# The order of SyncE's opening loads, the place of the key and query weights' measuring in layer 1, and the last tile's transposes one step later

## The chip, the cores and the metric

The kernel runs on one core of one Trainium2 chip. The metric is the device time of one execution in microseconds (us), the median of several runs. Names used below: PE is the tensor engine, ACT the scalar engine, DVE the vector engine, POOL the GpSimd engine, SP the sync engine, whose only work here is to issue DMA loads and stores. An engine with a q behind its name (SPq, ACTq) in the profile is that engine's instruction queue issuing a DMA.

## What is computed

Two layers of an encoder over 2048 tokens of width 1024, in float32. Each layer normalises the tokens, projects them with one combined matrix, mixes one half of the channels by a gated unit within chunks of 128 tokens and the other half by attention (8 query heads, 2 key/value heads, head width 64), projects back, normalises and adds.

```python
for l in range(DEPTH):
    h = rmsnorm(x, pre_g[l])
    proj = jnp.einsum('bsd,de->bse', h, w_in[l])
    u_a, v_a, g_a, q, k, v, g_b = jnp.split(proj, idx, axis=-1)
    y_a = gmlp_group(u_a, v_a, ln_a_g[l], ln_a_b[l], spatial_w[l], spatial_b[l]) * jax.nn.silu(g_a)
    y_b = gqa_axial_attention(q, k, v, q_norm_g[l], k_norm_g[l], tables) * jax.nn.silu(g_b)
    y = jnp.concatenate([y_a, y_b], axis=-1)
    out = jnp.einsum('bse,ed->bsd', y, w_out[l])
    x = x + rmsnorm(out, post_g[l])
```

`gqa_axial_attention` normalises queries and keys per head with `q_norm_g` and `k_norm_g`, rotates them by their row and column, and takes a softmax over all 2048 keys.

## The kernel before

**Numbers.** Every float32 operand of a matmul is split into a high and a low float16 part, and a product is three matmuls: high x high, low x high, high x low. A weight block has to be measured first (`split_steps`): its size gives a power of two, `w.e`, by which it is scaled before it is split. Measuring is done by a reduction of the raw block (`w_raw`) into columns of `w_col`; in the opening, half of it is done by squares on ACT instead, whose scratch result is called `fb`. Then come a small matmul `pe` that spreads the sum over the partitions, the scale `w_col<-g_col,w_col`, and eight pieces that write `w_hl`: high on ACT (or DVE), low on DVE (or POOL).

**Tokens.** The 2048 tokens are worked in 4 groups (`g`) of 4 tiles (`j`) of 128. A tile `x_t` is loaded, its squares are summed on ACT (`sq`, `ss_x`), a chain of tiny DVE instructions forms the reciprocal root (`rs_m` to `rs_x`; for two tiles at once `rr`), ACT scales one half of the tile and POOL the other, PE transposes it (`pt`), and ACT and DVE write the high and low half of `hT`. The projection matmuls are called `pp`.

**Order of blocks.** `run` goes through a list of blocks (weight block, group): first the two gate blocks `gb0` and `gb1` for each group, then keys and values with the first query block, and so on. Each call of `proj_tok` ticks a list of background jobs (`bg`) after each of its three passes of 8 matmuls; a job added with a delay of n runs at the n-th tick from then, at most 4 (later 2) to a tick. So a delay is a place in PE's program. In attention, `units` are pairs of a query tile and a key/value head; jobs hang on a step count `k` of 16 steps to a unit, 512 in all.

**Pinned and free instructions.** An instruction issued through the wrappers `PE`, `ACT`, `DVE`, `POOL` (class `Pinned`) keeps the place that the program gives it on its engine. One issued through `nc.vector`, `nc.scalar` or `nc.sync` is free: the scheduler may put it earlier or later in the engine's row. All SP loads are free before the change. Within its row each engine runs strictly in order. Each DMA sets one of eight completion semaphores, DMAHW0 to DMAHW7, that are handed round, and the next DMA on the same semaphore waits for it.

**The opening** is written out by hand at the end of `encoder` (line 1443 on): tile 0 and the gains of the pre-norm on SP, the first weight block (`w_first[0]`, two halves of 4 x 128 rows) on SP, the other three tiles of group 0 and the two halves of the second block on ACT's queue. Loads for group 1, the key weights and the six small loads of the query and key norm gains (`gains`, lines 249 to 259; three for each) come from background jobs of `run`, and `lng`, a gain of 512 elements of 4 bytes each, from `spatial_weights`.

**The boundary of the layers.** Layer 0's last tile is finished while layer 1's first projection already runs: `attend` ends by hanging its transposes `py`, its 12 products `pout` and its normalisation on background ticks 1 to 12 and later (line 1430 on). `o_tok` is that tile's attention result, divided by the softmax sums (`rden`). The measuring of layer 1's key and query weights (`split_w`, called by `split` in `run`) is free in layer 1 and pinned in layer 0. Layer 1's gains are asked for at step 256 of layer 0's attention and scaled (`scale_gains`, first instruction `g_top`) at step 268.

Of the kernel before, what the change touches and what calls it, by code (L numbers as in the profile page):

```python
# [19 lines left out]
P = 128  # L20
# [8 lines left out]
WB = 256  # L29
# [14 lines left out]
def encoder(ctx: ExitStack, tc, x, w_in, w_out, pre_g, post_g, ln_a_g, ln_a_b,  # L44
            spatial_w, spatial_b, q_norm_g, k_norm_g, rope, out):
    nc = tc.nc
# [43 lines left out]
            return f  # L90

    PE, ACT, DVE, POOL = Pinned(nc.tensor), Pinned(nc.scalar), Pinned(nc.vector), Pinned(nc.gpsimd)

    ident = const.tile([P, P], F32, name="ident")
    make_identity(nc, ident)
# [103 lines left out]
    class Project:  # L199
# [10 lines left out]
        def norm_row(self):  # L210

            self.g_col = lay.tile([P, ND], F32, name="g_col")
            self.g_row = f_t("fa")[0:ND, 0:P]
            nc.sync.dma_start(self.g_row, pre_g[self.l].rearrange("(d p) -> d p", p=P))

        def norm_turn(self):

# [4 lines left out]
        def begin(self):  # L222

            self.w_first = [Obj(), Obj()]
            steps = []
            for n, w in enumerate(self.w_first):
                raw = w_t([P, ND, WB], "w_raw", F32)

                def load(i, raw=raw, c=C_GB + n * WB, queue=ACT if n else nc.sync):
                    ds4 = slice(4 * i, 4 * i + 4)  # L230
                    queue.dma_start(raw[:, ds4], w_in[self.l, 4 * i * P:(4 * i + 4) * P, c:c + WB]
                                      .rearrange("(d p) e -> p d e", p=P))
                steps.append(([load], self.split_steps(w, raw, sums=4)))
            return steps
# [15 lines left out]
        def gains(self):  # L250
            l = self.l
            self.gain_q = lay.tile([P, 2, HD], F32, name="gain_q")
            self.gain_k = lay.tile([P, 2, HD], F32, name="gain_k")
            for gain, src in ((self.gain_k, k_norm_g), (self.gain_q, q_norm_g)):
                nc.sync.dma_start(gain[:, 0, :], src[l].partition_broadcast(P))
                gv = gain[:, 1, :].rearrange("p (a h i) -> p a h i", a=2, h=2)
                sv = src[l].rearrange("(a h i) -> a h i", a=2, h=2)
                for h in range(2):
                    nc.sync.dma_start(gv[:, :, h, :], sv[:, 1 - h, :].partition_broadcast(P))

        def scale_gains(self, v):
            top = small.tile([P, 2], F32, name="g_top")
# [12 lines left out]
        def spatial_weights(self):  # L275
            l = self.l
            self.lng = lay.tile([P, 4], F32, name="lng")
            nc.sync.dma_start(self.lng, ln_a_g[l].rearrange("(t p) -> p t", p=P))
            self.zbias = lay.tile([P, 4, P], F32, name="zbias")
            wsT = row_t("wsT")  # L280
            self.ws = row_t("ws", (P, 2, NH * P), F16)
            sq = small.tile([P, 4], F32, name="ws_sq", bufs=1)
            for hf in range(2):
                raw = f_t("fa")
                nc.sync.dma_start(raw.rearrange("p (g j) -> p g j", g=4),
                                  spatial_w[l, 4 * hf:4 * hf + 4].rearrange("g i j -> i g j"))

                def t(hf=hf, raw=raw):
                    ps = ps_t("pt")
                    for g in range(4):  # L290
                        PE.transpose(ps[:, g * P:(g + 1) * P], raw[:, g * P:(g + 1) * P], ident)
                    nc.scalar.copy(wsT[:, hf * GRP:(hf + 1) * GRP], ps)
                    nc.scalar.activation(raw, raw, AF.Square, accum_out=sq[:, hf:hf + 1])
                bg.add(WS_DELAY + 2 * hf, t)

            def scale():
                nc.vector.tensor_scalar(sq[:, 2:3], sq[:, 0:1], sq[:, 1:2], W_SPREAD, ALU.add, ALU.mult)
                ps = ps_t("pe")
                PE.matmul(ps[:, 0:1], ones, sq[:, 2:3], start=True, stop=True)
                top_scale(sq[:, 2:3], ps[:, 0:1], nc.vector, float(157 << 23))  # L300
                nc.vector.tensor_scalar(sq[:, 3:4].bitcast(I32), sq[:, 2:3].bitcast(I32), -1.0, float(254 << 23),
                                        ALU.mult, ALU.add)
                nc.vector.tensor_scalar(self.lng, self.lng, sq[:, 3:4], 1.0 / V_SCALE, ALU.mult, ALU.mult)

            def split(hf):
                sl = slice(hf * GRP, (hf + 1) * GRP)
                nc.scalar.activation(self.ws[:, 0, sl], wsT[:, sl], AF.Copy, scale=sq[:, 2:3])
                nc.vector.scalar_tensor_tensor(self.ws[:, 1, sl], wsT[:, sl], sq[:, 2:3], self.ws[:, 0, sl],
                                               ALU.mult, ALU.subtract)
            bg.add(WS_DELAY + 10, scale)  # L310
            for hf in range(2):
                bg.add(WS_DELAY + 20 + 4 * hf, lambda hf=hf: split(hf))
            lnb = f_t("fb")
            nc.sync.dma_start(lnb, ln_a_b[l].partition_broadcast(P))
            sb = f_t("fc").rearrange("p (c i) -> p c i", c=4)
            for h in range(2):
                src = spatial_b[l].rearrange("(c h) i -> h c i", h=2)[h]
                nc.sync.dma_start(sb[h * HD:(h + 1) * HD], src.partition_broadcast(HD))

            def bias():  # L320
                ps = ps_t("pt").rearrange("p (c i) -> p c i", c=4)
                for c in range(4):
                    for h in range(2):
                        e = (2 * c + h) * HD
                        PE.matmul(ps[h * HD:(h + 1) * HD, c], lnb[:, e:e + HD], wsT[:, 2 * e:2 * e + P],
                                  start=True, stop=True)
                nc.vector.tensor_tensor(self.zbias, ps, sb, ALU.add)
            bg.add(WS_DELAY + 14, bias)
# [96 lines left out]
        def hT_jobs(self, g):  # L425
# [4 lines left out]
            act, dve = (nc.scalar, nc.vector) if done else (ACT, DVE)  # L430
            parts = small.tile([P, TPG, 2], F32, name="ss_x", bufs=2)

            def load(j, queue=nc.sync):
                if done:
                    src = h_d[(g - 1) * TPG + j]
                    xs[j] = xt = [f_t("x_h") for _ in range(2)]
# [307 lines left out]
        def run(self, kv, first, last_jobs, first_wo):  # L744
# [42 lines left out]
                raws[name] = self.load_w(cols[name])  # L787

            def split(name, delay):
                w[name] = self.split_w(raws.pop(name), delay, self.l == 0 and name in ("kv", "q0"))  # L790

            def block(name, g):
                assert all(w[n].ready for n in (("va0", "va1") if name == "va" else (name,)))
# [117 lines left out]
    def attend(l, kv, nxt):  # L911
# [500 lines left out]
        def run(fs):  # L1412
            for f in fs:
                f()
# [16 lines left out]
        run(post_queue)  # L1431
        for n, f in enumerate(gb_pieces):
            bg.add(1 + n, f)
        bg.add(1, trans)
        bg.add(1, split)
        bg.add(4, lambda: run(mms[0] + after[0] + gain_part(s, 0, POOL)))
        bg.add(7, lambda: run(mms[1] + after[1] + gain_part(s, 1, POOL)))
        bg.add(10, lambda: run(posts[:4]))
        bg.add(11, lambda: run(posts[4:8]))
        for n, f in enumerate(posts[8:]):  # L1440
            bg.add(12 + n, f)

    layers = [Project(l) for l in range(DEPTH)]
    pj = layers[0]
# [3 lines left out]
    (loads, steps), (loads2, steps2) = pj.begin()  # L1448
    loads[0](0)
    loads[0](1)  # L1450
    pj.norm_turn()
    jobs.squares(0)
    for j in range(1, TPG):
# [4 lines left out]
    jobs.scale(0, z)  # L1458
    steps[2]()
    banks = [jobs.turn(0, 0)]  # L1460
    loads2[0](0)
    jobs.squares(1)
    steps[3]()
    banks.append(jobs.turn(0, 1))
# [8 lines left out]
    z = jobs.chain(1)  # L1473
    for d in (ND - 2, ND - 1):
        w.low(d, POOL)
    loads2[0](1)
    jobs.squares(2)
    jobs.scale(1, z)
    jobs.squares(3)
# [61 lines left out]
```

## Time and profile before

| | us |
|---|---|
| median of 3 runs | 2470.33 (2467.57, 2470.33, 2476.21) |
| the profiled execution | 2471.2 |
| its span, first to last instruction | 2469.2 |
| PE busy | 2414.1 (98%) |
| DVE / ACT / POOL busy | 1742.6 / 1639.0 / 1192.8 |
| granted PE clock, mean | 0.997 |
| DMA, mean rate | 76 GB/s |

The page divides the span into 40 slices of some 62 us; PE is at nine tenths or more in all but the first and the last two. A busy share is an average, so the stretches in which PE is not busy have to be looked for. The views used below: busy time by stretch (one line has, after the stretch and its length, busy us and instruction count of PE, PE's weight loads, DVE, ACT and POOL, then the granted clock, the DMA engines' share and GB/s); waits (who waited for whom: us in total, times, longest); and the timeline (start, length, engine, line, operation, output<-inputs; in brackets the idle time before it and what ended that). Line 89 is the wrapper of pinned instructions, so there the tile names tell which instruction it is.

### The profile page before, as it was taken

The page shows a single profiled execution, that of the slowest core. Times are in us where ns is not written, and L with a number is a line of the kernel's source. Part 1 is how long each engine was busy: PE and PEld are TensorE (multiplying, and loading weights), DVE is VectorE, ACT ScalarE, POOL GpSimd, SP SyncE. Part 2 cuts the span into 40 slices and gives each one's busy share as a digit, 9 for nine tenths or more (in the row PEclk, how much of TensorE's full clock was granted, in tenths as well). Part 3 has the DMA queues.
Part 4 walks back from the last instruction along what each step waited for, and adds up shares of the span by engine and source line. Part 5 has one row for each costly group of instructions (what it writes and reads, how often), then busy time and mean ns, then how long its engine had stood idle before and what let it go on. Part 6 is the DMA issues. An engine that isn't in the chain of part 4 may idle for free. (4 is left out here: it accounts for less than half of the span.)

```text
span 2469.2 us, 62843 instructions
## 1 busy us (share of the span) xinstructions
PE 2414.1 (98%) x25327; PEld 1600.1 (65%) x25327; DVE 1742.6 (71%) x4001; ACT 1639.0 (66%) x3545; POOL 1192.8 (48%) x1000
## 2 busy tenths in 40 slices
PE   5999999999999999999999999999999999999997
PEld 4988776445666666666579987764456666666664
DVE  5678566876678777777766875678667777777674
ACT  5665323247888888888854742231588888888886
POOL 2200110026777777777731111100477777777776
PEclk9999999999999999999999999999999999999999
DMA  5353213222121222111144422221321121212120
GB/s 175 123 175 89 59 49 92 61 80 73 52 92 40 62 66 70 60 48 64 57 150 147 144 69 69 74 62 57 107 66 38 50 61 42 68 43 68 51 68 27
DMA packets 174916, 188.11 MB, mean 76 GB/s; under 512 B 19608, under 2 KB 143648, under 8 KB 174624
## 3 DMA queue, kind: packets, MB, share of 16 engines
q1 hardware_dynamic: 173136, 181.47, 24.2%
q8 instruction: 198, 3.24, 0.5%
q10 hardware_dynamic: 1488, 2.62, 0.3%
q14 instruction: 94, 0.77, 0.1%
HBM read 129.38 MB, written 54.66 MB: 75 GB/s over the span
## 5 line engine op out<-in xcount | busy, mean ns | idle before, releaser
L89 POOL TENSOR_TENSOR p_parts<-p_f,p_parts 128x512 f16<-128x512 f32 x872 | 1034.2, 1198 | 331.5 <-ACT p_f L89 252.3
L89 ACT ACTIVATE p_parts<-sp 128x512 f16<-128x512 f32 x1024 | 620.2, 606 | 173.6 <-PE sp L89 125.4
L89 PEld LDWEIGHTS <-p_parts 128*128 128x128 f16 x12288 | 509.5, 97 | 249.7 <-POOL p_parts L89 6.5
L89 DVE TENSOR_REDUCE mx<-pmax 128x1 f32<-128x512 f32 x800 | 541.6, 684 | 177.1 <-PE pmax L89 174.0
L89 PE MATMUL pp<-w_hl,hT 128*128 128x256 f16 x5376 | 619.6, 274 | 5.4 <-ACT w_hl L89 5.0
L89 ACT ACTIVATE p_f<-sp 128x512 f32<-128x512 f32 x1024 | 617.7, 603 | 0.0
L89 PEld LDWEIGHTS <-hT 128*128 128x128 f16 x5376 | 526.3, 98 | 72.5 <-issue 3.5
L89 PE MATMUL po<-v_st,p_parts 128*128 128x65 f16 (+1 forms) x12288 | 542.4, 193 | 6.8 <-POOL p_parts L89 4.5
L89 PE MATMUL pout<-wo,y_t 128*128 128x512 f16 x1536 | 488.0, 378 | 1.7 <-ACT y_t L89 1.7
L89 PE MATMUL sp<-q,k_t 66*128 66x512 f16 x1024 | 390.0, 381 | 0.0
L89 PE MATMUL sp<-q_st,k_t 128*128 128x512 f16 x1024 | 387.8, 379 | 1.6 <-DVE o_tok L89 1.3
L89 PE MATMUL pmax<-k_t,q_m 128*128 128x512 f16 x1024 | 386.9, 379 | 0.8 <-DVE mx L89 0.4
L89 PE MATMUL pp<-hT,w_hl 128*128 128x512 f16 x1536 | 370.3, 379 | 0.0
L89 PEld LDWEIGHTS <-y_t 128*128 128x128 f16 x1536 | 148.9, 97 | 177.7 <-ACT y_t L89 3.3
L89 PEld LDWEIGHTS <-w_hl 128*128 128x128 f16 x1536 | 149.7, 98 | 174.0
L89 PEld LDWEIGHTS <-q_m 128*128 128x128 f16 x1024 | 101.1, 99 | 120.7
L971 DVE TENSOR_REDUCE mx<-pmax 128x1 f32<-128x512 f32 x224 | 150.3, 686 | 36.9 <-PE pmax L89 36.7
L89 POOL TENSOR_TENSOR wo<-wo_raw,wo 128x512 f16<-128x512 f32 x32 | 37.1, 1158 | 263.9 <-ACT wo L89 150.4
L89 DVE TENSOR_TENSOR p_parts<-p_f,p_parts 128x512 f16<-128x512 f32 x152 | 118.5, 780 | 36.8 <-ACT p_f L89 35.9
L628 POOL TENSOR_TENSOR fl<-fv,fh 128x512 f16<-128x512 f32 x32 | 38.0, 1206 | 205.7 <-ACT fh L627 197.0
L89 PEld LDWEIGHTS <-k_t 128*128 128x128 f16 (+1 forms) x2048 | 131.3, 97 | 3.8 <-DVE o_tok L89 1.4
L546 ACT ACTIVATE fc<-pp,rs_y 128x64 f32<-128x64 f32 x320 | 69.9, 355 | 69.5 <-DVE rs_y L123 69.5
(212 smaller groups left out, 2041.2 us busy)
## 6 DMA issues: line engine op xcount, KB each, us to landing
w_raw<-in_w_in_dram SPq DMA_DIRECT2D x10, 1024.0 KB
w_raw<-in_w_in_dram SPq DMA_DIRECT2D x18, 512.0 KB
gb_d<-fa SPq DMA_DIRECT2D x32, 256.0 KB
wo_row<-in_w_out_dram SPq DMA_DIRECT2D x16, 512.0 KB
wo_raw<-in_w_out_dram SPq DMA_DIRECT2D x16, 512.0 KB
z_d<-fb SPq DMA_DIRECT2D x32, 256.0 KB
fb<-z_d SPq DMA_DIRECT2D x32, 256.0 KB
ya_d<-fa SPq DMA_DIRECT2D x32, 256.0 KB
```

The lines of the kernel that those rows point to most:

```text
L89: return tc.keep_in_program_order(call(*args, **kw))
L546: nc.scalar.activation(qn[:, t, h], src[:, t, h], AF.Copy, scale=rs[:, i, t, h:h + 1])
L628: nc.gpsimd.tensor_tensor(s.lo, vh, s.hi, ALU.subtract)
L971: dve.tensor_reduce(s.mx[:, j, c:c + 1], ps, AX.X, ALU.max)
```

## The change

Three edits and what they bring along:

1. A fifth wrapper, `SP`, pins loads on the sync engine: the pre-norm gains, both first weight blocks (the second moves from ACT's queue to SP's), the query and key norm gains, `lng`, and the token tiles of groups 0 and 1 in layer 0. In the opening, both halves of the second weight block are issued directly behind those of the first.
2. The key weights' and first query block's measuring and splitting is pinned in layer 1 too.
3. The last tile's transposes, products and normalisation at the boundary come one background tick later.

```diff
+    SP = Pinned(nc.sync)
...
-            nc.sync.dma_start(self.g_row, pre_g[self.l].rearrange("(d p) -> d p", p=P))
+            SP.dma_start(self.g_row, pre_g[self.l].rearrange("(d p) -> d p", p=P))
...
-                def load(i, raw=raw, c=C_GB + n * WB, queue=ACT if n else nc.sync):
+                def load(i, raw=raw, c=C_GB + n * WB, queue=SP):
...
             for gain, src in ((self.gain_k, k_norm_g), (self.gain_q, q_norm_g)):
-                nc.sync.dma_start(gain[:, 0, :], src[l].partition_broadcast(P))
+                SP.dma_start(gain[:, 0, :], src[l].partition_broadcast(P))
...
-                    nc.sync.dma_start(gv[:, :, h, :], sv[:, 1 - h, :].partition_broadcast(P))
+                    SP.dma_start(gv[:, :, h, :], sv[:, 1 - h, :].partition_broadcast(P))
...
-            nc.sync.dma_start(self.lng, ln_a_g[l].rearrange("(t p) -> p t", p=P))
+            SP.dma_start(self.lng, ln_a_g[l].rearrange("(t p) -> p t", p=P))
...
-            def load(j, queue=nc.sync):
+            def load(j, queue=SP if self.l == 0 and g < 2 else nc.sync):
...
-                w[name] = self.split_w(raws.pop(name), delay, self.l == 0 and name in ("kv", "q0"))
+                w[name] = self.split_w(raws.pop(name), delay, name in ("kv", "q0"))
...
-        bg.add(1, trans)
-        bg.add(1, split)
-        bg.add(4, lambda: run(mms[0] + after[0] + gain_part(s, 0, POOL)))
-        bg.add(7, lambda: run(mms[1] + after[1] + gain_part(s, 1, POOL)))
-        bg.add(10, lambda: run(posts[:4]))
-        bg.add(11, lambda: run(posts[4:8]))
+        bg.add(2, trans)
+        bg.add(2, split)
+        bg.add(5, lambda: run(mms[0] + after[0] + gain_part(s, 0, POOL)))
+        bg.add(8, lambda: run(mms[1] + after[1] + gain_part(s, 1, POOL)))
+        bg.add(11, lambda: run(posts[:4]))
+        bg.add(12, lambda: run(posts[4:8]))
         for n, f in enumerate(posts[8:]):
-            bg.add(12 + n, f)
+            bg.add(13 + n, f)
...
     loads[0](0)
     loads[0](1)
+    loads2[0](0)
+    loads2[0](1)
     pj.norm_turn()
...
     banks = [jobs.turn(0, 0)]
-    loads2[0](0)
     jobs.squares(1)
...
-    loads2[0](1)
     jobs.squares(2)
```

SP's row from the start of the program, before, with the semaphores that a load waits for (`x_t` a token tile, `fa` the pre-norm gains, `w_raw` a weight block: 128x4x256 half of one of the first two, 128x8x256 the whole key block):

```order
L442 DMA x_t<-in_x_dram 128x1024
L214 DMA fa<-in_pre_g_dram 8x128
L231 DMA w_raw<-in_w_in_dram 128x4x256 x2
L255 DMA gain_k<-in_k_norm_g_dram 128x64
L259 DMA gain_k<-in_k_norm_g_dram 128x2x16 x2
L255 DMA gain_q<-in_q_norm_g_dram 128x64
L259 DMA gain_q<-in_q_norm_g_dram 128x2x16 [waits DMAHW0_49]
L259 DMA gain_q<-in_q_norm_g_dram 128x2x16 [waits DMAHW1_49]
L278 DMA lng<-in_ln_a_g_dram 128x4x1 [waits DMAHW2_49]
L442 DMA x_t<-in_x_dram 128x1024 [waits DMAHW6_49]
L442 DMA x_t<-in_x_dram 128x1024 [waits PE_49,DMAHW0_49,Activation_49,Pool_49]
```

The same place of the change:

```order
L89 DMA x_t<-in_x_dram 128x1024
L89 DMA fa<-in_pre_g_dram 8x128
L89 DMA w_raw<-in_w_in_dram 128x4x256 x4
L89 DMA x_t<-in_x_dram 128x1024 [waits DMAHW1_49]
L339 DMA w_raw<-in_w_in_dram 128x8x256 [waits DMAHW2_49]
L89 DMA x_t<-in_x_dram 128x1024 [waits DMAHW0_49,PE_49,DMAHW3_49,Activation_49,Pool_49]
L89 DMA gain_k<-in_k_norm_g_dram 128x64 [waits DMAHW4_49]
L89 DMA gain_k<-in_k_norm_g_dram 128x2x16 [waits DMAHW5_49]
L89 DMA gain_k<-in_k_norm_g_dram 128x2x16 [waits DMAHW6_49]
L89 DMA gain_q<-in_q_norm_g_dram 128x64 [waits DMAHW7_49]
```

The second weight block has moved up, the six gain loads have moved behind two tiles of group 1 and the key weights, and `lng` is gone from here.

ACT's row in the opening, before, behind the squares of tile 0 (`fb` is the measuring of the first weight half; the last row belongs to tile 1):

```order
L89 DMA x_t<-in_x_dram 128x1024 [waits DMAHW3_49]
L89 DMA x_t<-in_x_dram 128x1024 [waits DMAHW4_49]
L89 DMA x_t<-in_x_dram 128x1024 [waits DMAHW5_49]
L89 ACTIVATE fb,w_col<-w_raw,g_col 128x256 [waits DMAHW2_49,DVE_49]
L89 ACTIVATE fb,w_col<-w_raw,g_col 128x256 x3
L89 ACTIVATE x_t<-x_t,rs_x 128x512 [waits DVE_49]
L89 DMA w_raw<-in_w_in_dram 128x4x256 [waits DMAHW7_49]
L89 ACTIVATE sq,ss_x<-x_t 128x512 [waits DMAHW3_49]
```

And of the change:

```order
L89 DMA x_t<-in_x_dram 128x1024 x3
L89 ACTIVATE fb,w_col<-w_raw,g_col 128x256 [waits DMAHW2_49,DVE_49]
L89 ACTIVATE fb,w_col<-w_raw,g_col 128x256 x3
L89 ACTIVATE x_t<-x_t,rs_x 128x512 [waits DVE_49]
L89 ACTIVATE sq,ss_x<-x_t 128x512 [waits DMAHW6_49]
```

The three tile issues wait for no semaphore of another load any more, and the weight issue between them and tile 1's squares is gone.

DVE's row at the boundary of the layers, before (`rs_m`, `rs_o` begin the normalisation of the last tile but one; `rden` to `o_tok` finish the last tile):

```order
L89 TENSOR_SCALAR rs_o<-rs_m 128x1
L357 TENSOR_REDUCE w_col<-w_raw 128x4 x2
L361 TENSOR_TENSOR w_col<-w_col,g_col 128x8
L362 TENSOR_REDUCE w_col<-w_col 128x1
L368 TENSOR_SCALAR w_col<-w_col 128x1
L89 TENSOR_SCALAR rden<-po,cols 128x4
L89 RECIPROCAL rden<-rden 128x4
```

And of the change:

```order
L89 TENSOR_SCALAR rs_m<-ss_o,cols 128x1
L89 TENSOR_SCALAR rs_o<-rs_m 128x1
L89 TENSOR_SCALAR rden<-po,cols 128x4
L89 RECIPROCAL rden<-rden 128x4
L89 TENSOR_TENSOR gb<-gb,rden 128x2x2x64
```

The measuring of the key weights has left this place; it now stands after the first two gate products of layer 1 for group 0, ahead of group 1's token chain. Two more moves have no rows here: layer 1's six gain loads now stand in SP's row behind the `gb` load of step 256 of layer 0's attention (before, they stood among the projections of layer 0), and `lng` stands in each layer directly ahead of the loads for the spatial bias and the first rotation rows (`rope`).

## The prediction

> **What bounds the kernel now.** I read the page first, then busy time by stretch, then what the tensor engine waited for, then the timeline where it waited.
>
> ```profile
> span 2469.2 us, 62843 instructions
> PE 2414.1 (98%) x25327; PEld 1600.1 (65%) x25327; DVE 1742.6 (71%) x4001; ACT 1639.0 (66%) x3545; POOL 1192.8 (48%) x1000
> ...
> 0.00:50.00 50.00, 23.66 (x148) 17.60 (x149) 26.90 (x89) 26.79 (x68) 10.41 (x14) 0.95 0.59 192
> 100.00:200.00 100.00, 100.00 (x927) 90.31 (x925) 70.19 (x245) 59.98 (x168) 15.18 (x10) 1.00 0.48 146
> 1200.00:1300.00 100.00, 94.38 (x1053) 72.14 (x1052) 62.35 (x155) 69.47 (x147) 48.00 (x41) 1.00 0.36 117
> ```
>
> The first number after a stretch's length is PE busy. PE works through the whole program except in two places that this change touches: 26 of the first 50 us, and 5.6 us around the boundary of the layers. An edit elsewhere can only cost; an edit here is worth the PE idle time that it removes, since PE then works at 100% behind it.
>
> ```profile
> PE pt L89 <- ACT x_t L89: 15.3, 3, 13.1
> PE pp L89 <- ACT w_hl L89: 5.0, 3, 3.0
> ...
> PE py L89 <- DVE o_tok L89: 2.7, 1, 2.7
> ```
>
> PE's longest wait is 13.1 us for the first token tile, scaled on ACT; the 2.7 us are the last tile's transposes at the boundary. The opening, in order of time (start, length, engine; in brackets idle before and its end):
>
> ```profile
> 0.73 0.39 SPq L442 DMA_DIRECT2D x_t<-in_x_dram  x1
> ...
> 2.57 0.51 SPq L255 DMA_DIRECT2D gain_k<-in_k_norm_g_dram  x1
> ...
> 4.23 0.60 ACT L89 ACTIVATE sq<-x_t 128x512 f32<-128x512 f32 x1 [2.22 <-DMA x_t<-in_x_dram]
> ...
> 5.52 0.19 ACT L89 ACTIVATION_READ_ACCUMULATOR sq<-x_t 128x1 f32 x1
> ...
> 7.67 0.37 SPq L278 DMA_DIRECT2D lng<-in_ln_a_g_dram  x1
> ...
> 9.01 5.53 ACTq L89 DMA_DIRECT2D x_t<-in_x_dram  x3
> 9.01 1.22 DVE L89 TENSOR_REDUCE w_col<-w_raw 128x4 f32<-128x1024 f32 x1 [1.20 <-DMA w_raw<-in_w_in_dram]
> ...
> 14.64 0.51 ACT L89 ACTIVATE fb<-w_raw,g_col 128x256 f32<-128x256 f32 x1 [8.94 <-DMA x_t<-in_x_dram]
> ...
> 16.63 0.71 ACT L89 ACTIVATE x_t<-x_t,rs_x 128x512 f32<-128x512 f32 x1
> ...
> 17.39 1.11 PE L89 MATMUL pt<-ident,x_t 128*128 128x128 f32 x4 [13.06 <-ACT x_t L89]
> ...
> 19.33 0.23 DVE L89 TENSOR_SCALAR w_col<-g_col,w_col 128x8 f32<-128x8 f32 x1
> ...
> 20.25 0.60 ACT L89 ACTIVATE sq<-x_t 128x512 f32<-128x512 f32 x1 [2.91 <-DMA x_t<-in_x_dram]
> ...
> 22.10 0.91 ACT L89 ACTIVATE w_hl<-w_raw,w_col 128x256 f16<-128x256 f32 x2
> ...
> 24.12 0.20 DVE L89 TENSOR_SCALAR rs_m<-ss_x 128x1 f32<-128x1 f32 x1
> ```
>
> ACT is free at 5.71 us. Next in its order stand three issues of token tiles, and each waits for the semaphore of a load issued eight loads earlier: the second weight half (landed at 9.01, when DVE's reduction starts) and two of the small gain loads. So ACT measures the first weight half (fb) only at 14.64, though that half had landed by 7.67: the lng issue waits for its semaphore. The DMA engines were not the reason:
>
> ```profile
> 9.00:10.00 1.00, 0.00 (x0) 0.00 (x0) 0.99 (x1) 0.00 (x0) 0.56 (x1) 1.00 0.06 7
> ...
> 17.00:18.00 1.00, 0.61 (x3) 0.62 (x4) 0.38 (x2) 0.34 (x1) 0.00 (x0) 1.00 0.89 353
> ```
>
> The last two numbers are the DMA share and GB/s: 7 GB/s in the stall, 353 in a full microsecond.
>
> **The opening, step by step.** The written SP order has no gain load ahead of the token tiles, so ACT's three issues wait for nothing. They begin at 5.71 and take 3 x 0.43 = 1.3 us, to 7.0. fb then starts when its half lands, 7.65: 7.0 us earlier than 14.64. Its squares, the scaling of the tile and PE's first transposes move by the same 7.0 (17.39 to 10.4); DVE's reduction stays at 9.01 and is done in time. The weight scale, ready at 19.56, is ready at 12.6. ACT's squares of tile 1, which waited 2.91 us for its load, can begin at 10.35, so ACT's first w_hl goes from 22.10 to 12.6. DVE's four w_hl take 1.55 us and the two low halves of hT 0.69 each: DVE reaches the second tile's chain at 15.6 instead of 24.12, which is **8.5 us**. What follows waits for DVE and ACT in a pinned order, not for loads, and keeps that distance.
>
> The condition is tile 1's landing. Squares to chain take 24.12 - 20.25 = 3.87 us, so it may land as late as 11.7; each later microsecond costs one. The bounds: tile 0 took 3.5 us from issue to landing (0.73 to 4.23), which gives 9.2; tile 1 before took 11.2 us (9.01 to 20.25), which gives 16.9 and leaves 3.3 us of gain. I take the near end, since the long one fell into the idle DMA microseconds quoted. Counted by bytes: tile 0 and the first weight block are in by 9.0; tile 1 and as much of the second block are 1.05 MB, 3 us at 353 GB/s, so 12 if nothing of them had moved before, and about 11 since both stand in the queues by then.
>
> On this a rule bears: the Trainium skill, "DMA: Bandwidth & Descriptors", section "Issuing engines are not separate DMA queues", says that loads issued on ACT and SP run on the same 16 DMA engines, so that a second issuing engine saves only issue time. By it the second weight block's move to SP is worth nothing, and its 1 MB, now issued ahead, competes with tile 1; the sum would be the same 8.5 with shared bandwidth, less with the tile behind the block. No row before has both.
>
> The moves that I cost at nothing, with their cover. The six gain loads go behind the second tile of group 1; their first reader was at 59.6 us, DVE's scale_gains, and three such loads take some 7 us (below). The second block's ACT issues (0.4 us each) vanish beside a waiting ACT.
>
> **The clock.** The granted clock (the number before the DMA share) is not full in the opening:
>
> ```profile
> 36.00:40.00 4.00, 4.00 (x29) 3.28 (x28) 1.78 (x3) 2.52 (x8) 0.00 (x0) 0.76 0.35 115
> 48.00:52.00 4.00, 3.82 (x20) 2.66 (x20) 2.89 (x17) 3.97 (x13) 0.00 (x0) 0.57 0.17 57
> ```
>
> Lost there: 4 x 0.24 + 4 x 0.43 = 2.7 us. The same gaps between the same matmuls stay, so I take no change, with 2 us either way. The Trainium skill, "TensorE: Matmul & The Clock Gate", section "Part 1: The HAM clock gate (the "warmup" mystery)", has the activity window run free, so the same gaps can meet it otherwise; that fits a term without a sign.
>
> **The boundary.**
>
> ```profile
> 1240.02 7.23 SPq L338 DMA_DIRECT2D w_raw<-in_w_in_dram  x2
> ...
> 1246.35 0.83 PE L89 MATMUL po<-v_st,p_parts 128*128 128x65 f16 x12
> 1246.49 2.34 DVE L357 TENSOR_REDUCE w_col<-w_raw 128x4 f32<-128x1024 f32 x2 [2.54 <-DMA w_raw<-in_w_in_dram]
> ...
> 1249.40 0.21 DVE L89 TENSOR_SCALAR rden<-po,cols 128x4 f32<-128x4 f32 x1
> ...
> 1250.32 0.42 DVE L89 TENSOR_TENSOR o_tok<-po,gb 128x256 f32<-128x256 f32 x1
> ...
> 1250.80 0.44 PE L89 MATMUL py<-ident,o_tok 128*128 128x128 f32 x2 [2.74 <-DVE o_tok L89]
> ```
>
> DVE had put the measuring of layer 1's key weights ahead of the last tile: it waited for them, reduced them, and reached rden at 1249.40, while po was complete at 1247.2. Pinned, the measuring stands after the first projection block. rden to the end of o_tok takes 1.34 us, so o_tok is ready at 1248.6. PE runs 16 matmuls (2.1 us from 1247.0) instead of 8 ahead of the transposes, to 1249.1: no wait, **2.7 us** gained, and 0.5 spare. Were the extra tick handed on to the product of the last tile, 1.0 of it would go, so 1.7 to 2.7. The pinned splits of layer 1 then alternate with transposes as layer 0's already do, where PE was busy 100.00 of 100 us.
>
> The gain loads of layer 1 now stand in the middle of layer 0's attention, behind this gb load; the second fence is three of them and the DMA rate after:
>
> ```profile
> 893.15 0.35 SPq L1284 DMA_DIRECT2D gb<-gb_d  x1
> ...
> 924.64 0.34 DVE L89 TENSOR_REDUCE g_top<-gain_k 128x1 f32<-128x64 f32 x2
> ```
>
> ```profile
> 417.11 1.30 SPq L255 DMA_DIRECT2D gain_q<-in_q_norm_g_dram  x1
> 418.46 0.94 SPq L259 DMA_DIRECT2D gain_q<-in_q_norm_g_dram  x2
> ...
> 423.00:424.00 1.00, 1.00 (x10) 0.82 (x9) 0.69 (x1) 0.00 (x0) 0.00 (x0) 1.00 0.06 7
> ```
>
> The trickle lasts from 417 to 424, 7 us for three, so 14 for six: landed by 908, read at 924.64, 17 us spare. The q loads behind them serve step 272, four after g_top's, and have the same cover. Nothing. lng, now in front of the rope rows, delays these; they had slack:
>
> ```profile
> 1357.01 1.27 POOL L528 TENSOR_TENSOR fa<-fa,gain_k 128x512 f32<-128x512 f32 x1 [35.39 <-DMA fa<-in_rope_dram]
> ...
> 1363.20 0.43 DVE L548 TENSOR_TENSOR fc<-fc,fa 128x256 f32<-128x256 f32 x1 [0.39 <-ACT fc L546]
> ```
>
> POOL ends at 1358.3, DVE reads at 1363.2: 4.9 us of cover, so nothing, at worst 2 us a layer by a trickle of 7 us.
>
> **The sum.** 8.5 + 2.7 = 11.2 us off the profiled execution's 2471.2 us (span 2469.2 and 2.0 around it) gives **2460.0**. That execution is 0.9 us above the median, 2470.33; the three timed runs spread over 8.6 us.
>
> **Rivals.** One, the issue itself is slow:
>
> ```profile
> L89 ACTq DMA_DIRECT2D x_t<-in_x_dram x3: 387/434/3510, 9.0 to 11.0; - x3
> ```
>
> One of ACT's three issues took 3.51 us in itself. If the group takes 5.53 us again, from 5.71, fb starts at 11.3, 3.3 us earlier; with tile 1 there by then, DVE's chain starts at 19.3 instead of 24.12: 4.8, and 2463.7 in all. For it: that issue shows no wait of its own. Against: the gain loads were then unfinished, and SP's issues take 0.4.
>
> Two, tile 1 comes late, behind the second weight block on the shared engines: it lands at 16.9, the opening gives 3.3, the total is 6.0: 2465.2.
>
> Three, slower than before: the gain loads in mid-attention hold SP. If each of the six holds the queue for 7.23 us, as the pair of loads at 1240.02 did, the last is issued at 893.5 + 43 = 937 and lands 2.3 us later (7 us for three), at 939; DVE stands 15 us at scale_gains, with the maxima and subtractions that PE needs behind it, and the sum is 2471.2 - 11.2 + 15 = 2475. It costs from a landing past 924.6 on, makes the kernel slower than before past 936, and by over 0.3% past 943; 14 us of trickle were measured where 31 are free, so it is unlikely.
>
> Four, nothing of it shows: other waits close up behind both places, 2471.
>
> **Chances.** Forecast 0.60, slow issue 0.15, late tile 0.14, nothing 0.06, slower 0.05 (one in five of that within 0.3%). The range goes from 2455 (clock and spread on the good side) to 2468 (the late tile, with the spread). A measurement of this kernel tells about 0.3% from no change, 7.4 us: below 2462.9 is faster. That takes nearly all of the forecast and part of rivals one and two: faster 0.68, same 0.28, slower 0.04.
>
> **What would show it.** In the opening: ACT's three issues directly behind the squares of tile 0, fb near 7.7, PE's first transposes near 10.4, tile 1's squares with no wait, PE's first pp near 13. At the boundary: no measuring between rs_o and rden on DVE, py without idle time ahead. In attention: g_top without a wait for a gain load. Wrong it would be if fb started after 10 us, if DVE's second chain came after 18, or if PE showed a new wait between 890 and 940 us or behind either place.

## The result and the profile after

| | before | changed |
|---|---|---|
| median of 5 runs, us | 2469.75 (2467.57 to 2476.21) | 2460.90 (2460.81 to 2465.39) |
| the profiled execution, us | 2471.2 | 2460.9 |
| its span, us | 2469.2 | 2459.1 |

The ratio is 0.9966, 95% interval 0.9950 to 0.9982: the changed kernel is faster by 0.34%. The medians lie 8.9 us apart, and the interval allows 4.4 to 12.3. The forecast was 2460.0 us.

Busy time by stretch of the changed kernel (columns as before: stretch, length, busy us of PE, PE's loads, DVE, ACT, POOL, granted clock, DMA share, GB/s):

```profile
0.00:50.00 50.00, 34.25 (x234) 26.80 (x235) 33.49 (x117) 34.07 (x84) 16.59 (x18) 0.97 0.62 206
100.00:200.00 100.00, 100.00 (x926) 89.94 (x925) 70.25 (x242) 56.91 (x168) 8.77 (x7) 1.00 0.48 143
1200.00:1300.00 100.00, 98.63 (x1056) 78.17 (x1055) 65.29 (x163) 67.79 (x143) 42.05 (x36) 1.00 0.40 135
```

PE works 34.25 of the first 50 us instead of 23.66, and 98.63 of the 100 us around the boundary instead of 94.38. The opening, in order of time:

```profile
1.59 2.14 SPq L89 DMA_DIRECT2D w_raw<-in_w_in_dram  x4
4.86 1.11 ACTq L89 DMA_DIRECT2D x_t<-in_x_dram  x2
6.00 0.69 ACTq L89 DMA_DIRECT2D x_t<-in_x_dram  x1
7.78 0.51 ACT L89 ACTIVATE fb<-w_raw,g_col 128x256 f32<-128x256 f32 x1 [2.21 <-DMA w_raw<-in_w_in_dram]
10.52 1.12 PE L89 MATMUL pt<-ident,x_t 128*128 128x128 f32 x4 [5.87 <-ACT x_t L89]
11.94 0.60 ACT L89 ACTIVATE sq<-x_t 128x512 f32<-128x512 f32 x1 [1.47 <-DMA x_t<-in_x_dram]
12.63 0.23 DVE L89 TENSOR_SCALAR w_col<-g_col,w_col 128x8 f32<-128x8 f32 x1
14.35 1.01 PE L89 MATMUL pp<-w_hl,hT 128*128 128x256 f16 x4 [1.37 <-ACT w_hl L89]
15.81 0.20 DVE L89 TENSOR_SCALAR rs_m<-ss_x 128x1 f32<-128x1 f32 x1
```

ACT's three issues of token tiles are done at 6.69 (before: 14.54). fb starts at 7.78 (14.64) and now waits for its own weights, not for an issue. One thing that the prediction did not have is in row six: ACT still waits 1.47 us for tile 1. DVE's second chain, the last row, begins at 15.81 instead of 24.12: 8.3 us earlier.

The boundary:

```profile
1236.79 0.83 PE L89 MATMUL po<-v_st,p_parts 128*128 128x65 f16 x12
1237.45 1.91 PE L89 MATMUL pp<-w_hl,hT 128*128 128x256 f16 x16
1237.66 0.22 DVE L89 TENSOR_SCALAR rden<-po,cols 128x4 f32<-128x4 f32 x1 [3.26 <-PE po L89]
1238.59 0.42 DVE L89 TENSOR_TENSOR o_tok<-po,gb 128x256 f32<-128x256 f32 x1
1239.20 0.38 PE L89 MATMUL py<-ident,o_tok 128*128 128x128 f32 x2
```

DVE stands idle 3.26 us and takes rden as soon as po is there; o_tok ends at 1239.01, and PE reaches py behind 16 products at 1239.20 with no idle time in brackets. In attention the gain loads of layer 1 are issued 30 us ahead of their reader, which waits for nothing:

```profile
883.97 1.42 SPq L89 DMA_DIRECT2D gain_k<-in_k_norm_g_dram  x3
885.43 1.45 SPq L89 DMA_DIRECT2D gain_q<-in_q_norm_g_dram  x3
...
915.09 0.34 DVE L89 TENSOR_REDUCE g_top<-gain_k 128x1 f32<-128x64 f32 x2
```

### The profile page after: what moved, and what is told of

Same layout as the page of the kernel before. It is cut to its first block, busy times and chain, and to the rows that moved or that the text cites. A ratio compares the mean times of both kernels' runs of the same rounds, so it can differ in the third digit from the quotient of the medians.

```text
span 2459.1 us, 62836 instructions
## 1 busy us (share of the span) xinstructions
PE 2415.6 (98%) x25327; PEld 1600.6 (65%) x25327; DVE 1743.1 (71%) x4001; ACT 1638.0 (67%) x3545; POOL 1190.1 (48%) x1000
```

## Experiments

Each profile is one execution. The table puts the marks of all of them side by side: start of fb, of ACT's squares of tile 1 and of DVE's second chain; PE's wait for o_tok at the boundary; the granted clock's loss in the opening (16 to 60 us) and later (60 to 2436), summed over stretches of 4 us as 4 x (1 - clock); the start of PE's last `py`, some 16 us ahead of the end; and that less the loss. A ratio is to the kernel before, measured beside it.

| kernel | median us | ratio, 95% interval | fb | tile 1 | chain | py wait | clock loss | last py | less loss |
|---|---|---|---|---|---|---|---|---|---|
| before | 2469.75 | | 14.64 | 20.25 | 24.12 | 2.74 | 3.4 / 0 | 2453.7 | 2450.3 |
| changed | 2460.90 | 0.9966 (0.9950-0.9982) | 7.78 | 11.94 | 15.81 | 0 | 1.7 / 1.7 | 2442.6 | 2439.2 |
| e9_changed_again | 2460.03 | 0.9963 (0.9951-0.9976) | 6.79 | 12.29 | 16.16 | 0 | 1.7 / 0 | 2441.1 | 2439.4 |
| e1_opening_only | 2463.32 | 0.9967 (0.9955-0.9979) | 7.14 | 11.90 | 15.77 | 3.59 | 0 / 6.8 | 2448.4 | 2441.6 |
| e2_boundary_only | 2466.12 | 0.9980 (0.9972-0.9988) | 13.32 | 19.39 | 23.25 | 0 | 0 / 0 | 2446.2 | 2446.2 |
| e3_gains_free | 2463.57 | 0.9971 (0.9960-0.9982) | 13.15 | 15.74 | 20.76 | 0 | 1.7 / 0 | 2445.4 | 2443.7 |
| e4_block2_behind_tiles | 2458.62 | 0.9951 (0.9937-0.9964) | 7.92 | 11.81 | 15.68 | 0 | 3.4 / 0 | 2444.6 | 2441.2 |
| e5_boundary_no_pin | 2461.99 | 0.9970 (0.9959-0.9981) | 8.21 | 12.37 | 16.24 | 2.54 | 3.4 / 3.4 | 2450.0 | 2443.1 |
| e6_boundary_no_tick | 2460.86 | 0.9964 (0.9950-0.9977) | 7.99 | 11.93 | 15.80 | 0.57 | 0 / 0 | 2439.1 | 2439.1 |
| e7_tile1_last | 2463.80 | 0.9977 (0.9967-0.9986) | 7.91 | 15.69 | 19.56 | 0 | 1.7 / 0 | 2444.5 | 2442.8 |
| e8_block2_as_before | 2459.72 | 0.9956 (0.9944-0.9969) | 7.45 | 11.33 | 15.20 | 0 | 3.4 / 0 | 2442.5 | 2439.1 |
| e10_tile1_first | 2459.43 | 0.9960 (0.9945-0.9975) | 8.18 | 10.77 | 15.79 | 0 | 3.4 / 0 | 2442.8 | 2439.4 |
| e11_tiles_held | 2461.11 | 0.9966 (0.9953-0.9979) | 6.15 | 10.69 | 14.55 | 0 | 1.7 / 3.4 | 2444.0 | 2438.9 |

### The two parts apart

`e1_opening_only`, the changed kernel with:

```diff
-                w[name] = self.split_w(raws.pop(name), delay, name in ("kv", "q0"))
+                w[name] = self.split_w(raws.pop(name), delay, self.l == 0 and name in ("kv", "q0"))
...
-        bg.add(2, trans)
-        bg.add(2, split)
+        bg.add(1, trans)
+        bg.add(1, split)
```

and so on for the other pieces. `e2_boundary_only` makes the opposite two edits in the kernel before.

> The changed kernel with its boundary part undone: the splits of layer 1's key and query weights are free again and the last tile's pieces come one tick earlier, as before. Theory (two gains that add): the opening reads as in the changed kernel (fb near 7.8 us, second chain near 15.8), and at the boundary PE waits 2.7 us for o_tok again, so the time is 2460.9 + 2.7 = 2463.6 us and the span some 2.7 us over the changed kernel's, give or take what the clock and the last store add (1 to 2 us). Rival (the boundary's gain is taken back further on, so that only the opening counts): the wait of 2.7 us is there and the time is still near 2461.

> The kernel before with the boundary part alone: pinned splits in layer 1, one tick later. Theory: the opening as before (fb 14.6, second chain 24.1), no idle time of PE ahead of the last tile's py, measuring of the key weights behind the first projection block; 2469.8 - 2.7 = 2467.1 us. Rival: PE's 2.7 us come back as other waits between there and layer 1's attention, 2469.8 us; then the shift of layer 1's first v_row product against the boundary's py would be smaller than 2.7 us.

The boundary of e1 in its timeline, and its clock there:

```profile
1238.31 2.35 DVE L358 TENSOR_REDUCE w_col<-w_raw 128x4 f32<-128x1024 f32 x2 [3.38 <-DMA w_raw<-in_w_in_dram]
1241.21 0.21 DVE L89 TENSOR_SCALAR rden<-po,cols 128x4 f32<-128x4 f32 x1
1242.61 0.69 PE L89 MATMUL py<-ident,o_tok 128*128 128x128 f32 x2 [3.59 <-DVE o_tok L89]
```

```profile
1240.00:1244.00 4.00, 1.39 (x7) 1.08 (x8) 3.61 (x14) 0.66 (x2) 0.00 (x0) 0.70 0.66 230
1244.00:1248.00 4.00, 4.00 (x20) 2.82 (x19) 3.43 (x8) 0.91 (x3) 0.00 (x0) 0.50 0.32 131
```

The measuring stands ahead of rden again, and PE waits 3.59 us, more than before since the key weights landed later against po: the reduction starts 0.99 us behind the start of the last po (1237.32), before 0.14. In this execution the clock then went to half. Less the clock's loss, e1's last py comes 2.4 us behind the changed kernel's, 2.7 expected. The median is 2.4 us above it too, but the ratio to the kernel beside it, 0.9967, is that of the changed kernel, 0.9966: the timed runs do not tell e1 from its rival, the trace does. e2 has no wait at py, and less the loss its last py comes 4.1 us earlier than before, so nothing gives the boundary's gain back. But its median lies 0.20% below before, 4.9 us (3.0 to 6.9), more than the 2.7 expected: in its profile the opening, whose code is that of before, also came 0.9 us earlier. The medians of the parts add up to more than the whole, within their intervals; the traces are the better measure here.

### What the boundary's part consists of

`e5_boundary_no_pin` undoes only the first line of e1's diff, `e6_boundary_no_tick` only the ticks.

> The changed kernel with the splits of layer 1's key and query weights free again, but with the later tick kept. Theory (the boundary's 2.7 us are two parts, 1.7 from the measuring that leaves DVE's place ahead of the last tile and 1.0 from eight more products ahead of the transposes): DVE measures the key weights ahead of rden again, o_tok is as late as before, PE waits 1.7 us for it (2.6 if o_tok comes 3.6 us late, as it did with the opening alone); time 2460.9 + 1.7 = 2462.6. Rival (the tick alone does it): no wait at py, 2460.9.

> The changed kernel with the pinned splits kept and the later tick undone. Theory: o_tok ends 1.7 us after the last po of layer 0 is done, and PE has eight products (1.0 us) to do in that time, so it waits 0.6 to 0.8 us at py; time 2460.9 + 0.7 = 2461.6. Rival (the pinning alone does it all): no wait at py, 2460.9.

The same row, py, first of e5, then of e6:

```profile
1244.24 0.44 PE L89 MATMUL py<-ident,o_tok 128*128 128x128 f32 x2 [2.54 <-DVE o_tok L89]
```

```profile
1236.11 0.44 PE L89 MATMUL py<-ident,o_tok 128*128 128x128 f32 x2 [0.57 <-DVE o_tok L89]
```

With neither edit PE waits 2.74 or 3.59 us, with the tick alone 2.54, with the pin alone 0.57, with both nothing. So the pin carries it and the tick takes the rest. Without the pin the tick is worth 1.05 us (e1 against e5, which differ by it alone), with the pin 0.57. Both rivals fall, by one trace each. The medians do not show 0.6 us.

### Why ACT's issues were held

`e3_gains_free`, the changed kernel with:

```diff
-                SP.dma_start(gain[:, 0, :], src[l].partition_broadcast(P))
+                nc.sync.dma_start(gain[:, 0, :], src[l].partition_broadcast(P))
...
-                    SP.dma_start(gv[:, :, h, :], sv[:, 1 - h, :].partition_broadcast(P))
+                    nc.sync.dma_start(gv[:, :, h, :], sv[:, 1 - h, :].partition_broadcast(P))
```

> The changed kernel with only the six gain loads left free on SP, so that the order puts them ahead of the token tiles again; both blocks of the first weights still go out early on SP. Theory (ACT's issues of the token tiles wait for semaphores of the gain loads): ACT's three issues end late again, fb starts at 13 to 15 us instead of 7.8, the second chain at 22 to 24 instead of 15.8, and the time is 2460.9 plus 7 to 10, 2468 to 2471. Rival A (the early second block on SP brought the gain): fb stays near 7.8 and the time at 2461. Rival B (an issue of ACT is slow in itself): fb and time as in the changed kernel, or fb moved by no more than 3.5 us, the length of that issue before.

In the order, the six gain loads then stand behind the two weight blocks and ahead of the tiles. ACT's three issues of e3, one by one, and fb:

```profile
6.71 0.38 ACTq L89 DMA_DIRECT2D x_t<-in_x_dram  x1
...
11.92 0.33 ACTq L89 DMA_DIRECT2D x_t<-in_x_dram  x1
...
12.77 0.33 ACTq L89 DMA_DIRECT2D x_t<-in_x_dram  x1
13.15 0.51 ACT L89 ACTIVATE fb<-w_raw,g_col 128x256 f32<-128x256 f32 x1 [7.50 <-DMA x_t<-in_x_dram]
```

The issues end at 13.10 and fb starts at 13.15. So the place of the gain loads decides, and neither rival is left: the second block is early here too, and no issue of ACT takes over 0.4 us. But the chain comes at 20.76, not at 22 to 24, the time is 2463.57, not 2468 to 2471, and the gain loads hold ACT by their number more than by their own landing. The semaphores are handed round eight to a turn, and with two weight loads ahead the tiles fall on others.

```
L89 DMA x_t<-in_x_dram 128x1024 [waits DMAHW2_49]
L89 DMA x_t<-in_x_dram 128x1024 [waits DMAHW5_49]
L89 DMA x_t<-in_x_dram 128x1024 [waits DMAHW6_49]
```

These are ACT's three issues in e3's order; before they waited for DMAHW3, 4 and 5, and in the changed kernel for none. DMAHW2 belongs to the first half of the first weight block, DMAHW5 to the second half of the second block, DMAHW6 to the first gain load. By the semaphore events of e3's trace these landed at 6.69, 11.90 and 12.75, and each issue starts 0.02 us behind. So the wait for a weight half costs 4.8 us here (7.09 to 11.92), the wait for a gain load 0.5. The same three issues before:

```profile
9.01 0.39 ACTq L89 DMA_DIRECT2D x_t<-in_x_dram  x1
9.44 0.43 ACTq L89 DMA_DIRECT2D x_t<-in_x_dram  x1
11.03 3.51 ACTq L89 DMA_DIRECT2D x_t<-in_x_dram  x1
```

The first starts when the second weight half has landed (8.99), the second right behind it, the third when the second gain load has (11.01). Of the 8.83 us from 5.71 to 14.54, then, 3.30 are the wait for a weight half, 1.16 the wait for a gain load, 3.51 the third issue itself and 0.86 the other two. What made the third issue long, no run shows; in e2, which has the same opening, it took 1.82 us.

In e3 tile 1 goes out at 6.71, not at 9.01, and its squares have no wait. So 5.0 of the 8.3 us come back with the gains' place alone; the rest needs the second weight block behind the tiles as well, as before. The load of `lng`, which also left the opening, was not tested apart.

### The second weight block

`e8_block2_as_before`: the changed kernel with the second block's two loads on ACT at their old places. `e4_block2_behind_tiles` puts them on ACT right behind the three tiles:

```diff
-    loads2[0](0)
-    loads2[0](1)
     pj.norm_turn()
     jobs.squares(0)
     for j in range(1, TPG):
         jobs.load(j, ACT)
+    for i in range(2):
+        loads2[0](i, queue=ACT)
```

> The changed kernel with the second weight block's two loads back on ACT's queue at their places of before (behind the scaling of tile 0, and behind the first w_hl), the gain loads staying late. Theory (with the gain loads out of the way ACT's three issues wait for nothing wherever the second block is, and that block is not needed before 25 us): ACT's issues in 1.1 to 1.6 us, fb at 7.1 to 7.9 us, the second chain at 15.0 to 15.9, the time 2461 within 1.5. Rival (the early second block is a part of the gain by itself, as the 3.3 us could say that stayed gained with the gain loads ahead): a wait for the second block appears ahead of its measuring, and the time is 2463 to 2464.

> The changed kernel with the second weight block's two loads issued by ACT right behind its three token tiles, no longer by SP ahead of them. Theory (the second block ahead of tile 1 delays it on the shared DMA engines, and its place matters for nothing else): fb stays at 7.7 to 8.2 us, tile 1's squares lose their wait of 1.47 us and start near 10.5, the second chain comes at 14.6 to 15.0 instead of 15.8, PE's first w_hl product near 13.4; time 1 us lower, 2460. Rival (the issue order does not decide when tile 1 lands): tile 1's squares still at 11.9 and the chain at 15.8, time 2461. If the second block's later arrival costs, a wait for it stands ahead of DVE's measuring of that block, and the time is above 2461.

Tile 1's squares, first of e8, then of e4:

```profile
11.33 0.60 ACT L89 ACTIVATE sq<-x_t 128x512 f32<-128x512 f32 x1 [1.20 <-DMA x_t<-in_x_dram]
```

```profile
11.81 0.60 ACT L89 ACTIVATE sq<-x_t 128x512 f32<-128x512 f32 x1 [1.20 <-DMA x_t<-in_x_dram]
```

e8 went by its theory: the block's move to SP's queue is worth nothing, and with the block at its old place the chain still comes at 15.20 instead of 24.12. In e4 the theory fell: with the block behind the tiles, tile 1's squares start at 11.81, as in the executions of the changed opening (11.90 to 12.37). SP's queue was not left empty there, though: its next load, a tile of group 1, went out at 2.58 instead of 4.29. e4's lower median, 2.3 us under the changed kernel's, is not borne out: the intervals of the ratios overlap, and in its trace, of the slowest of its six executions, the last py comes 2.0 us later even less the clock's loss.

### What tile 1 waits for

`e7_tile1_last` turns ACT's loop round, `for j in (3, 2, 1)`. `e10_tile1_first` is e4 with `jobs.load(1, ACT)` ahead of `jobs.squares(0)`. `e11_tiles_held` is e8 with:

```diff
-    for j in range(1, TPG):
-        jobs.load(j, ACT)
+    jobs.load(1, ACT)
...
     jobs.scale(0, z)
+    for j in (2, 3):
+        jobs.load(j, ACT)
```

> The changed kernel with ACT's three issues in the order tile 3, 2, 1, so that 1.05 MB of its own queue go ahead of tile 1. Theory (transfers under way share the engines, and tile 1 lands with the crowd, whatever its place in the queue): tile 1's squares at 11.5 to 12.8 us, the second chain 3.87 us behind them, time 2461 within 1.5. Rival (they are served in the order of issue): tile 1 lands 1.05 MB / 0.4 MB per us = 2.6 us later, squares at 14.5, chain at 18.4, time 2463.5. In both, each microsecond that tile 1 is later moves the chain by one.

> The changed kernel with tile 1 issued by ACT before its first squares, near 0.8 us instead of 4.9, and the second weight block issued by ACT behind tiles 2 and 3. Theory (shared engines): tile 1 is there before it is wanted (squares of tile 1 without wait, right behind the scaling of tile 0), but its 0.5 MB lie beside the first weight block, so fb starts up to 1.4 us later, 7.9 to 9.3; the chain then follows fb: fb + 6.5 to 8 us, 15 to 16.5; time 2461 within 1.5. Rival (the first weight block is limited by its own transfer): fb at 7.1 to 7.9, squares without wait at 10.4, chain at 14.3 to 15, time 2460.

> The kernel with the second weight block at its old places on ACT, and besides tiles 2 and 3 issued by ACT only behind the scaling of tile 0, so that 1.05 MB fewer are under way with tile 1. Theory (tile 1 lands with the crowd): tile 1's squares start right behind ACT's issues, near 10.5, without a wait for the load (11.3 before with the wait), the chain at 14.3 to 14.8 instead of 15.2, time 2459 to 2460. Rival (tile 1's landing does not depend on the other tiles): squares still at 11.3 to 11.9, chain at 15.2 to 15.8.

e7 and e11:

```profile
15.69 0.60 ACT L89 ACTIVATE sq<-x_t 128x512 f32<-128x512 f32 x1 [5.09 <-DMA x_t<-in_x_dram]
...
19.56 0.20 DVE L89 TENSOR_SCALAR rs_m<-ss_x 128x1 f32<-128x1 f32 x1
```

```profile
6.15 0.51 ACT L89 ACTIVATE fb<-w_raw,g_col 128x256 f32<-128x256 f32 x1 [0.52 <-DVE rs_x L89]
...
10.69 0.60 ACT L89 ACTIVATE sq<-x_t 128x512 f32<-128x512 f32 x1 [1.85 <-DMA x_t<-in_x_dram]
...
14.55 0.20 DVE L89 TENSOR_SCALAR rs_m<-ss_x 128x1 f32<-128x1 f32 x1
```

Two tiles ahead of it in ACT's own queue make tile 1 3.75 us later (15.69 against 11.94): my theory that it lands with the crowd fell, and the place in its own queue decides. By the semaphore events the first tile of ACT's queue landed at 12.04 in e7 (tile 3) and at 11.92 in the changed kernel (tile 1). The rival, order of issue, had 14.5 for the squares, 1.2 us too early. Whether the second weight block stands ahead on the other queue or behind in its own made no difference (e4). The Trainium skill, "DMA: Bandwidth & Descriptors", section "Queues, rings and completion order", has each DMA engine go round the queues that have work, a packet at a time; that fits both, but no run left the other queue empty to show it. Holding tiles 2 and 3 back brings fb to 6.15 and tile 1 to 10.69, from 7.45 and 11.33 in e8. Among five executions of the changed opening fb differs by 1.4 us (6.79 to 8.21) and tile 1 by 0.5, so e11's step, from one trace, is only likely; against the theory, tile 1's squares still waited 1.85 us. Tile 1 issued first (e10) is there in time, but tile 0 then lands late (its squares start at 5.43 instead of 4.09), fb waits for tile 0's rs_x and starts at 8.18, and the chain is back at 15.79. That is the theory's time, but not its reason, which was a late weight block: the first weight half landed at 7.15, in the changed kernel at 7.70.

Wherever ACT waited for tile 1, DVE's second chain stands 3.86 or 3.87 us behind those squares. Where it did not (e3, e10), the chain stands 2.9 us behind the weight scale. In the changed kernel the scale (12.63) would give 15.55: the tile costs 0.26 us beyond that, and 1.1 in e9, the same code. So e11's opening is 1.3 us shorter than the changed kernel's, which no median here can tell; its ratio is the changed kernel's.

### The changed kernel once more

> The changed kernel once more, unchanged, for what differs from one execution to the next. Theory (the clock's drops of 1.7 us each, and 1.0 us behind the last store, are the execution's and not the change's): the gate's first anchors and py at the boundary stand within 0.3 us of the first profile wherever no drop of the clock lies between, the number and places of the drops differ, and the median is 2460.9 within 1.5 us. Rival (they belong to the change): a drop again near 1772 us, and the last store again 1 us longer than before.

e9 has no drop of the clock near 1772, and py of the boundary starts at 1238.88 instead of 1239.20; in the opening its one drop comes earlier (24 to 32 us instead of 36 to 44). So the drops are the execution's. The opening differs by more than the theory's 0.3 us: fb 1.0 us earlier, the chain 0.35 later. Against the theory, the last store again ended 16.5 us behind the last py, as in the first profile and not as before. The clock's stretches stand further down.

## Why the prediction was right

**The opening.** 8.5 us were forecast, by the order of ACT's issues; the chain moved by 8.3. fb (7.65 forecast), the transposes (10.4) and the weight scale (12.6) came within 0.13 us: 7.78, 10.52, 12.63. e3 and e8 show that the gain loads' place decides, e8 that the second block's move is not needed. The prediction named the right semaphores (the second weight half and two gain loads); of the 8.8 us for which ACT stood, these waits were 4.5 and the one long issue 3.5. The forecast counted that length as gone as well, and it went, but no run shows why: this part came right by luck. The three issues were expected from 5.71 to 7.0 and ran from 4.86 to 6.69, which changed nothing, since fb waited for its weights.

**Tile 1** was the condition: it might land up to 11.7, and each later microsecond would cost one. It was there at 11.94, and the chain was 0.2 us later than forecast. The byte count's "about 11" was about 1 us short. Rival two priced that landing at 16.9 behind the second weight block; e4 shows no delay by the block, and e8, without it, a landing 0.6 us earlier, close to what executions differ by. Rival one, which took the group's 5.53 us over, is out: the three took 1.83 in all. But single issues can be long after the change too: SP's tile of group 1 took 2.21 us at 4.29, which held up nothing. The Trainium skill's rule that the prediction cited ("DMA: Bandwidth & Descriptors", "Issuing engines are not separate DMA queues") holds for the block's move, worth nothing in e8.

**The boundary.** 2.7 us forecast. Layer 0's last po came 9.56 us earlier than before (1236.79 against 1246.35), layer 1's first x_h transposes 12.23 us earlier (1248.42 against 1260.65): 2.67 us. The share put on the tick, 1.0, measured 0.57 with the pin and 1.05 without. The spare of 0.5 us ahead of py was 0.2 (o_tok's end at 1239.01, py at 1239.20).

**The moves costed at nothing.** g_top has no wait, in layer 0 (49.66) nor in layer 1 (915.09). lng now stands ahead of the rope rows:

```profile
1344.98 1.27 POOL L529 TENSOR_TENSOR fa<-fa,gain_k 128x512 f32<-128x512 f32 x1 [32.00 <-DMA fa<-in_rope_dram]
1350.96 0.43 DVE L549 TENSOR_TENSOR fc<-fc,fa 128x256 f32<-128x256 f32 x1 [0.38 <-ACT fc L547]
```

POOL ends at 1346.25 and DVE reads at 1350.96: 4.7 us of cover, 4.9 before. Rival three never came near: the six loads in mid-attention were issued within 2.9 us, not 7.23 each.

**The clock** was the term without a sign. These stretches are of before (the one that the prediction did not quote), of the changed kernel, and of its repetition e9:

```profile
32.00:36.00 4.00, 2.84 (x17) 2.11 (x18) 2.81 (x6) 3.41 (x9) 3.11 (x2) 0.82 0.10 23
```

```profile
36.00:40.00 4.00, 2.43 (x10) 1.29 (x10) 2.89 (x10) 4.00 (x12) 0.00 (x0) 0.72 0.33 108
40.00:44.00 4.00, 4.00 (x34) 3.33 (x32) 2.98 (x17) 3.65 (x10) 1.32 (x1) 0.85 0.00 0
1768.00:1772.00 4.00, 2.49 (x31) 1.40 (x30) 3.86 (x9) 4.00 (x11) 2.68 (x3) 0.97 0.30 101
1772.00:1776.00 4.00, 4.00 (x34) 2.41 (x33) 2.06 (x5) 3.31 (x8) 4.00 (x4) 0.60 0.92 273
```

```profile
24.00:28.00 4.00, 3.09 (x14) 2.30 (x15) 2.34 (x5) 2.92 (x7) 3.10 (x2) 0.64 0.31 119
28.00:32.00 4.00, 4.00 (x37) 3.57 (x35) 2.62 (x4) 3.32 (x10) 0.00 (x0) 0.93 0.46 137
1772.00:1776.00 4.00, 3.86 (x61) 2.72 (x59) 2.76 (x4) 4.00 (x10) 3.89 (x5) 1.00 0.86 253
```

Before lost 3.4 us in its opening (the prediction had counted 2.7, without the stretch from 32), the changed kernel 1.7 there and 1.7 again in layer 1, where e9 lost nothing. So the two profiles lost the same, and the forecast of no change held between them by accident of that second drop. Less the loss, the last py moved by 11.1 us, and by 10.9 in e9: the sum of 11.2. The spans differ by 10.1 only, since the last store ended 1.0 us later against that py (2459.1 - 2442.6 = 16.5, before 2469.2 - 2453.7 = 15.5). e5 has the same code there and 15.4, so that is no cost of the change; what sets it stays open.

**The number** owes something to luck. The sum was taken off a profiled execution, 2471.2 us, which lay 1.4 us above the median of five; the medians moved by 8.9 us (by 10.8 in e9's runs), not by 11.2, so that from the median the same sum would have given 2458.6.

## What to carry to other kernels

When an engine that computes also issues loads, look up which earlier load's semaphore each issue waits for: small loads ahead that nobody needs yet use up the free semaphores, and the issue then waits for a load that it has nothing to do with (here 3.3 us for a weight half and 1.2 for a gain load, the latter with the DMA engines nearly idle). One load more or less ahead changes which. Split a group of issues into its single ones before naming what held it. Free work that waits for a load (here a measuring on DVE) should be pinned behind the work that PE waits for, even if it is itself urgent. With differences of a few us in 2460, add up single waits between anchors in the traces and take the clock's drops out; medians of five runs do not resolve parts below some 3 us.

## What was not expected of the hardware

The clock's loss comes in portions. In the two columns of the table it is 0, 1.7, 3.4 or 6.8 us, and each portion of 1.7 is some 3.4 us at half speed (1244 to 1248 in e1 shows 0.50 for a whole stretch). The Trainium skill, "TensorE: Matmul & The Clock Gate", section "Part 1: The HAM clock gate (the "warmup" mystery)", states half speed and a window of about 3.4 us that runs free; the portions agree. Where they fall is the execution's: the five kernels with the changed opening word for word (changed, e9, e1, e5, e6) lost 1.7, 1.7, 0, 3.4 and 0 us there. PE need not be idle for long: in the changed kernel the drop at 1772 came behind a stretch in which PE was busy 2.49 of 4 us and idle for 1.30 us at the longest, and e9, with 2.50 of 4, had none. Not explained is what is left between executions whose second chain starts within 1.1 us: less the loss, the last py of e4 and e5 came 2 to 4 us behind that of e6 and e8, of which the wait at py explains 2.5 in e5.

The length of an issue is not explained either: of 1058 in each of the 13 profiles, 22 to 30 took over 1 us, among them the 3.51 us on ACT before and the 2.21 us on SP in the changed kernel, while most of those shown here took 0.3 to 0.7.
